# Issuing the half-step products by width: 512-column matmuls first, then 256-column ones

## The chip, the cores and the metric

One Trainium2 chip, one of its cores. The metric is the device time of one execution in microseconds (us). The kernel before took 1057.5 us in the median of three runs (1057.06 to 1058.75).

## What is computed

A decoder trunk of two layers over 256 tokens of width 1024, in float32. Each layer is a half-step SwiGLU, a token mixer (multi-head latent attention in layer 0, forgetting attention in layer 1), a second half-step SwiGLU, and a gated per-layer embedding. The change touches the half-steps alone; there are four of them, and they are most of the arithmetic:

```
D_MODEL = 1024
SEQ = 256
D_FF = 2816

def rms_norm(x, g):
    return (x * lax.rsqrt(jnp.mean(x * x, axis=-1, keepdims=True) + EPS)) * g

def swiglu(x, w_in, w_out):
    gate, up = jnp.split(x @ w_in, 2, axis=-1)
    return (jax.nn.silu(gate) * up) @ w_out

for i in range(DEPTH):
    h = h + FFN_HALF * swiglu(rms_norm(h, g_ffn1[i]), ffn1_w_in[i], ffn1_w_out[i])
    ...                                   # the mixer
    h = h + FFN_HALF * swiglu(rms_norm(h, g_ffn2[i]), ffn2_w_in[i], ffn2_w_out[i])
    gate = jax.nn.sigmoid(rms_norm(h, g_ple[i]) @ ple_w_gate[i])
    h = h + gate * (p[i] @ ple_w_proj[i])
```

## The kernel before

Every operand of a large product is split into two float32r parts, a high one and a low one, and a product is the sum of three: high times high, high weights times low activations, low weights times high activations. An activation tile is laid out as `[128, k, 2, 256]`: for each block `k` of 128 rows the 256 high values and then the 256 low ones. So in a half-step two matmuls do the three products of a block: one streams all 512 columns (high and low) past the high weights (line 241), and one streams the 256 high columns past the low weights (line 242) into the second half of the same 512 columns of PSUM. The trace calls the high weights `whi`, the low ones `wlo`, the activations `xa` (normed input) or `hid` (hidden activations); it names a matmul's moving operand first and its stationary one second.

Weights come in units of 1 MB (eight blocks of 128 rows by 256 columns): SyncE loads a unit into one of three `raw` buffers (line 70); ScalarE copies it into `whi` (line 86) and VectorE subtracts into `wlo` (line 87), in two pieces of four blocks each; `whi` and `wlo` have six buffers each, which are three units. Splitting runs two units ahead of use. A buffer is free again when the last matmul that reads it is done.

A half-step (`ffn`) has two stages. In the first, for each of 11 values of `f`, `part` multiplies `xa` by a unit for the gate (`pg`) and by one for the up path (`pu`): per unit 8 blocks times 2 column groups of 128, so 16 pairs of matmuls, 352 pairs in a half-step. Each accumulates in a PSUM tile of two banks (`pa`, two buffers). ScalarE copies half of the tile out and VectorE adds the other half (`summed`), then come the silu, the product and the split into `hid`. In the second stage, for 4 groups of output columns, `hid` (22 blocks) is multiplied by units of 8, 8 and 6 blocks: 176 pairs in a half-step. The result is added to the residual `h`, and the next norm's `xa` is made of it chunk by chunk (lines 357 and 359); GpSimd sums the squares (lines 367 and 371), and line 377 or 389 spreads their sum with a matmul.

In all half-steps but the first, `f == 0` is issued so that chunks of `xa` may arrive late: blocks 0 to 5 for the gate, blocks 0 to 5 for the up path, then blocks 6 and 7 for the gate, the spreading matmul, blocks 6 and 7 for the up path. In the very first half-step `part` is called with two blocks at a time.

In the half-steps the matmuls stay in the order in which the program issues them (`steady`). VectorE's and ScalarE's instructions are placed by a scheduler, apart from the first few steps of each half-step.

Outside the half-steps, `mm_w` (lines 234 to 236) streams activations of 256 columns past weights, three matmuls to a block, and `mm_x` (lines 247 to 249) streams weights of 256, 384 or 512 columns past activations.

Of the kernel before, what the change touches and what calls it, by code (L numbers as in the profile page):

```python
# [16 lines left out]
P = 128  # L17
S = 256
D = 1024
KD = D // P  # L20
FF = 2816
KF = FF // P
# [129 lines left out]
def trunk(ctx: ExitStack, tc: tile.TileContext, a: dict, out: bass.AP):  # L152
    nc = tc.nc
# [75 lines left out]
    steady = Order(tc)  # L229
# [5 lines left out]
        steady(nc.tensor.matmul(ps, lhsT=hi, rhs=x[:, k, 1, :], start=False, stop=False, skip_group_check=True))  # L235
        return steady(nc.tensor.matmul(ps, lhsT=lo, rhs=x[:, k, 0, :], start=False, stop=stop, skip_group_check=True))  # L236

    def mm_wide(ps, wt, cols, x, k, start, stop):

        hi, lo = wt[0][:, cols], wt[1][:, cols]  # L240
        steady(nc.tensor.matmul(ps, lhsT=hi, rhs=x[:, k], start=start, stop=False, skip_group_check=True))  # L241
        return steady(nc.tensor.matmul(ps[:, 1, :], lhsT=lo, rhs=x[:, k, 0, :], start=False, stop=stop, skip_group_check=True))  # L242

    def mm_x(ps, wt, x, k, tt, start, stop):

# [6 lines left out]
    start = ExitStack()  # L252
# [26 lines left out]
    def small_loads():  # L279
# [22 lines left out]
        out=upper, in_=upper, compare_op=ALU.is_ge, fill=0.0, base=0, pattern=[[1, P]], channel_multiplier=-1  # L302
# [4 lines left out]
        out=mask[:, P:], in_=mask[:, P:], compare_op=ALU.is_ge, fill=NEG, base=0, pattern=[[-1, P]], channel_multiplier=1  # L307
# [23 lines left out]
    def tt_op(o, x, y, op):  # L331
        return nc.vector.tensor_tensor(o, x, y, op=op)  # L332
# [63 lines left out]
    def two(r):  # L396
        return r.unsqueeze(1).broadcast_to([P, 2, S])


    def wide():  # L400
        return pa().rearrange("p (b a t) -> p b a t", b=2, a=2)

    def part(ps, wt, x, ks):
        for k in ks:
            for b in range(2):
                last = mm_wide(ps[:, b], wt(k), slice(b * P, (b + 1) * P), x, k, start=(k == 0), stop=(k == KD - 1))
        return last.ins

    def ffn(norm, after, fpool, beside={}, opened=None):

        steady.on = True
        x = norm.x
        hid = fpool.tile([P, KF, 2, S], F32R, name="hid", tag="hid", bufs=1)
        r = rh = None
        def summed(ps, name):
            o = fpool.tile([P, 2, S], F32, name=name, tag=name)
            nc.scalar.copy(o, ps[:, :, 0, :])
            tt_op(o, ps[:, :, 1, :], o, ALU.add)
            return o
# [5 lines left out]
        def product(f, gt, hf):  # L425
            tt_op(hf, gt, hf, ALU.mult)
            nc.scalar.copy(hid[:, 2 * f : 2 * f + 2, 0, :], hf)
            return tt_op(hid[:, 2 * f : 2 * f + 2, 1, :], hf, hid[:, 2 * f : 2 * f + 2, 0, :].bitcast(F32), ALU.subtract)

        for f in range(KF // 2):  # L430
            if f == 0:
                if opened:
                    pg, pu, pieces, roots, copies = opened
                    gt = summed(pg, "gt")
                    for _ in pieces:
                        pass
                    first = gt, summed(pu, "hf")
                    roots()
                    beside[0](None, None)
                    continue  # L440
                else:
                    pg, wg = wide(), w.get()
                    pu, wu = wide(), w.get()
                    part(pg, wg, x, range(6))
                    part(pu, wu, x, range(6))
                    part(pg, wg, x, range(6, KD))
                    order.on = True
                    r = norm.spread()
                    last = part(pu, wu, x, range(6, KD))
            else:  # L450
                pg = wide()
                if f == 1 and opened:
                    w.get(), w.get()
                part(pg, w.get(), x, range(KD))
                if f == 1 and opened:
                    r = roots()
                    gate(first[0])
                    product(0, *first)
                    copies()
# [5 lines left out]
            if f:  # L465
                pu = wide()
                last = part(pu, w.get(), x, range(KD))
            hf = summed(pu, "hf")
            low = product(f, gt, hf)
# [4 lines left out]
        for dp in range(4):  # L474
            ps = wide()
            for k0 in range(0, KF, 8):
                wt = w.get()
                for k in range(min(8, KF - k0)):
                    for b in range(2):
                        mm_wide(  # L480
                            ps[:, b], wt(k), slice(b * P, (b + 1) * P), hid, k0 + k, start=(k0 + k == 0), stop=(k0 + k == KF - 1)
                        )
            ot = summed(ps, "ot")
            tt_op(ot, ot, two(rh), ALU.mult)
            c = slice(2 * dp, 2 * dp + 2)
            tt_op(h[:, c, :], h[:, c, :], ot, ALU.add)
            after.chunk(dp)
# [785 lines left out]
```

## Time and profile before

| what | value |
|---|---|
| median of three runs | 1057.5 us |
| the profiled execution's own time | 1056.91 us |
| its span, first to last instruction | 1055.2 us |
| TensorE (PE) busy | 1041.4 us, 99% |
| weight loads (PEld) busy | 920.8 us, 87% |
| VectorE (DVE) busy | 783.8 us, 74% |
| ScalarE (ACT) busy | 593.5 us, 56% |
| mean granted TensorE clock | 0.999 |

The profiled execution took 1056.91 us; 1.7 us of it lie around the span. Matmuls are pipelined: the profile draws each longer than the time it holds the array, so their busy times overlap and their sum is more than the span. What one matmul costs is read from start to start of neighbours in the timeline.

### The profile page before, as it was taken

Reading aid. Unit: us, or ns where it says so; the run is one execution under the profiler, and the core shown is the slowest. Engines: PE = TensorE matmul, PEld = TensorE weight load, DVE = VectorE, ACT = ScalarE, POOL = GpSimd, SP = SyncE. Lnnn points to the kernel's source line nnn. Section 1 sums busy time; section 2 is a strip of 40 time slices with the busy share of each in tenths; the row PEclk is TensorE's granted clock in tenths of the full one; section 3 lists DMA queues with packets and bytes.
Section 4 is the critical chain, followed back from the end, with each engine's and each line's share of the span. In section 5 each row is a group of like instructions: output and inputs, shape, how many; then the busy total and the mean of one; then the engine's idle time right before and its main releaser. Section 6 shows DMA issues by size and latency. Waiting matters only on the chain.

```text
span 1055.2 us, 16340 instructions
## 1 busy us (share of the span) xinstructions
PE 1041.4 (99%) x6380; PEld 920.8 (87%) x6380; DVE 783.8 (74%) x1369; ACT 593.5 (56%) x903; POOL 71.7 (7%) x99
## 2 busy tenths in 40 slices
PE   8999999999999999999999999999999999999998
PEld 7888888987898888889988888889998988888886
DVE  5988766679979777666987676658888797766665
ACT  6655554568765555455656555535655665554552
POOL 0000000133110000001110000001000200000010
PEclk9999999999999999999999999999999999999999
DMA  7765555525336665556546554654643356555541
GB/s 241 241 209 190 188 182 170 170 88 183 98 113 198 202 198 189 162 196 211 161 145 218 196 191 154 214 153 140 217 138 115 96 194 215 185 189 182 187 160 40
DMA packets 171105, 182.60 MB, mean 173 GB/s; under 512 B 6094, under 2 KB 164372, under 8 KB 171028
## 3 DMA queue, kind: packets, MB, share of 16 engines
q1 hardware_dynamic: 170452, 181.03, 53.1%
q8 instruction: 50, 0.82, 0.3%
q10 hardware_dynamic: 576, 0.53, 0.2%
q14 instruction: 27, 0.22, 0.1%
HBM read 180.50 MB, written 1.05 MB: 172 GB/s over the span
## 4 chain that ended last, share of the span: by engine, by line
PE 92%; DVE 3%; issue 2%; POOL 1%; ACT 1%; DMA 1%; ACTq 0%; DVEq 0%; POOLq 0%
PE pa L241 45%; PE pa L242 23%; PE pa L247 3%; PE pa L249 3%; PE pa L248 3%; PE pa L234 2%; PE pa L236 2%; PE pa L235 2%; PE pb L601 1%; DVE wlo L87 1%; PE pb L508 1%; PE pb L548 1%; PE pb L536 1%; DMA xn<-in_x_dram 1%; POOL sq L367 1%
## 5 line engine op out<-in xcount | busy, mean ns | idle before, releaser
L87 DVE TENSOR_TENSOR wlo<-raw,whi 128x1024 fp32r<-128x1024 f32 (+2 forms) x351 | 418.2, 1202 | 199.2 <-ACT whi L86 198.6
L86 ACT CAST whi<-raw 128x1024 fp32r<-128x1024 f32 (+2 forms) x351 | 352.6, 1016 | 318.9 <-PE pa L241 195.0
L241 PE MATMUL pa<-xa,whi 128*128 128x512 f32 x1408 | 497.4, 396 | 0.9 <-DVE xa L359 0.9
L242 PE MATMUL pa<-xa,wlo 128*128 128x256 f32 x1408 | 396.2, 281 | 0.0
L241 PEld LDWEIGHTS pa<-xa,whi 128*128 128x128 f32 x1408 | 265.4, 189 | 64.1 <-DVE xa L359 1.2
L242 PEld LDWEIGHTS pa<-xa,wlo 128*128 128x128 f32 x1408 | 264.6, 188 | 0.1
L241 PE MATMUL pa<-hid,whi 128*128 128x512 f32 x704 | 244.2, 393 | 0.0
L242 PE MATMUL pa<-hid,wlo 128*128 128x256 f32 x704 | 195.5, 278 | 0.0
L241 PEld LDWEIGHTS pa<-hid,whi 128*128 128x128 f32 x704 | 131.9, 187 | 30.2
L242 PEld LDWEIGHTS pa<-hid,wlo 128*128 128x128 f32 x704 | 132.3, 188 | 0.0
L367 POOL TENSOR_TENSOR sq<-sq 128x512 f32<-128x512 f32 x21 | 31.6, 1504 | 841.5 <-ACT sq L365 827.7
L247 PE MATMUL pa<-whi,xa 128*128 128x256 f32 (+3 forms) x192 | 58.9, 307 | 0.0
L249 PE MATMUL pa<-whi,xa 128*128 128x256 f32 (+3 forms) x192 | 57.5, 300 | 0.0
L248 PE MATMUL pa<-wlo,xa 128*128 128x256 f32 (+3 forms) x192 | 57.3, 298 | 0.0
L234 PE MATMUL pa<-xa,whi 128*128 128x256 f32 x184 | 54.2, 295 | 0.0
L236 PE MATMUL pa<-xa,wlo 128*128 128x256 f32 x184 | 51.9, 283 | 0.0
L235 PE MATMUL pa<-xa,whi 128*128 128x256 f32 x184 | 51.8, 282 | 0.0
L247 PEld LDWEIGHTS pa<-whi,xa 128*128 128x128 f32 x192 | 36.1, 188 | 1.4 <-issue 0.5
L423 ACT ACTIVATE gt<-gt 128x512 f32<-128x512 f32 x44 | 27.6, 627 | 16.8 <-DVE gt L332 16.8
L248 PEld LDWEIGHTS pa<-wlo,xa 128*128 128x128 f32 x192 | 36.2, 188 | 0.8
L249 PEld LDWEIGHTS pa<-whi,xa 128*128 128x128 f32 x192 | 36.1, 188 | 0.9
L234 PEld LDWEIGHTS pa<-xa,whi 128*128 128x128 f32 x184 | 34.5, 188 | 1.9 <-issue 1.4
(281 smaller groups left out, 1196.9 us busy)
## 6 DMA issues: line engine op xcount, KB each, us to landing
raw<-in_ffn_w_in_dram SPq DMA_DIRECT2D x86, 1024.0 KB, 5.1
raw<-in_ffn_w_out_dram SPq DMA_DIRECT2D x32, 1024.0 KB, 5.1
raw<-in_ffn_w_out_dram SPq DMA_DIRECT2D x16, 768.0 KB, 4.6
raw<-in_ple_w_gate_dram SPq DMA_DIRECT2D x8, 1024.0 KB, 5.2
raw<-in_fox_w_in_dram SPq DMA_DIRECT2D x8, 1024.0 KB, 6.0
raw<-in_mla_w_o_dram SPq DMA_DIRECT2D x4, 1024.0 KB, 5.0
raw<-in_fox_w_o_dram SPq DMA_DIRECT2D x4, 1024.0 KB
raw<-in_mla_w_in_dram SPq DMA_DIRECT2D x3, 1024.0 KB, 6.3
```

The lines of the kernel that those rows point to most:

```text
L86: self.order(self.nc.scalar.copy(h, whole))
L87: self.order(self.nc.vector.tensor_tensor(low, whole, h.bitcast(F32), op=ALU.subtract))
L234: steady(nc.tensor.matmul(ps, lhsT=hi, rhs=x[:, k, 0, :], start=start, stop=False, skip_group_check=True))
L235: steady(nc.tensor.matmul(ps, lhsT=hi, rhs=x[:, k, 1, :], start=False, stop=False, skip_group_check=True))
L236: return steady(nc.tensor.matmul(ps, lhsT=lo, rhs=x[:, k, 0, :], start=False, stop=stop, skip_group_check=True))
L241: steady(nc.tensor.matmul(ps, lhsT=hi, rhs=x[:, k], start=start, stop=False, skip_group_check=True))
L242: return steady(nc.tensor.matmul(ps[:, 1, :], lhsT=lo, rhs=x[:, k, 0, :], start=False, stop=stop, skip_group_check=True))
L247: steady(nc.tensor.matmul(ps, lhsT=x[:, k, 0, t], rhs=wt[0], start=start, stop=False, skip_group_check=True))
L248: steady(nc.tensor.matmul(ps, lhsT=x[:, k, 0, t], rhs=wt[1], start=False, stop=False, skip_group_check=True))
L249: steady(nc.tensor.matmul(ps, lhsT=x[:, k, 1, t], rhs=wt[0], start=False, stop=stop, skip_group_check=True))
L367: nc.gpsimd.tensor_tensor(sq, sq, self.acc, op=ALU.add)
L423: nc.scalar.activation(gt, gt, AF.Silu)
```

## The change

In the half-steps a unit's matmuls are issued in another order. Before, each block and column group had its 512-column matmul and then its 256-column one. After, all 512-column matmuls of the unit (or of the blocks of one call of `part`) come first, and then all 256-column ones. Number, shapes, operands and accumulation are the same. The new line 255 stands for the old 241, and the new 248 for the old 242.

```
-    def mm_wide(ps, wt, cols, x, k, start, stop):
-
-        hi, lo = wt[0][:, cols], wt[1][:, cols]
-        steady(nc.tensor.matmul(ps, lhsT=hi, rhs=x[:, k], start=start, stop=False, skip_group_check=True))
-        return steady(nc.tensor.matmul(ps[:, 1, :], lhsT=lo, rhs=x[:, k, 0, :], start=False, stop=stop, skip_group_check=True))
+    def by_width(pss, wt, x, ks, first, last, at=0):
+        out = None
+        for low in range(2):
+            for k in ks:
+                for b, ps in enumerate(pss):
+                    cols = slice(b * P, (b + 1) * P)
+                    if low:
+                        out = steady(
+                            nc.tensor.matmul(
+                                ps[:, 1, :], lhsT=wt(k)[1][:, cols], rhs=x[:, at + k, 0, :], start=False, stop=(k == last),
+                                skip_group_check=True,
+                            )
+                        )
+                    else:
+                        steady(
+                            nc.tensor.matmul(
+                                ps, lhsT=wt(k)[0][:, cols], rhs=x[:, at + k], start=(k == first), stop=False, skip_group_check=True
+                            )
+                        )
+        return out
...
     def part(ps, wt, x, ks):
-        for k in ks:
-            for b in range(2):
-                last = mm_wide(ps[:, b], wt(k), slice(b * P, (b + 1) * P), x, k, start=(k == 0), stop=(k == KD - 1))
-        return last.ins
+        return by_width([ps[:, b] for b in range(2)], wt, x, ks, 0, KD - 1).ins
...
                 wt = w.get()
-                for k in range(min(8, KF - k0)):
-                    for b in range(2):
-                        mm_wide(
-                            ps[:, b], wt(k), slice(b * P, (b + 1) * P), hid, k0 + k, start=(k0 + k == 0), stop=(k0 + k == KF - 1)
-                        )
+                by_width([ps[:, b] for b in range(2)], wt, hid, range(min(8, KF - k0)), -k0, KF - 1 - k0, k0)
```

TensorE at the start of the third half-step (layer 1, first one), before; `pa_5329` is the gate's PSUM tile, `xa_5101` the activations, `whi_5181` and `wlo_5182` the first piece of the gate's unit:

```order
L236 MATMUL pb_5260<-xa_3346,wlo_5115 128x256
L241 MATMUL pa_5329<-xa_5101,whi_5181 128x512
L242 MATMUL pa_5329<-xa_5101,wlo_5182 128x256
L241 MATMUL pa_5329<-xa_5101,whi_5181 128x512
L242 MATMUL pa_5329<-xa_5101,wlo_5182 128x256
```

The two widths alternate, and go on alternating to the end of the half-step. The same place after the change; `pa_5340` is the up path's tile, `whi_5185` and `wlo_5186` are the gate's second piece, and line 394 is the old 377:

```order
L236 MATMUL pb_5260<-xa_3346,wlo_5115 128x256
L255 MATMUL pa_5329<-xa_5101,whi_5181 128x512 x8
L255 MATMUL pa_5329<-xa_5101,whi_5185 128x512 x4
L248 MATMUL pa_5329<-xa_5101,wlo_5182 128x256 x8
L248 MATMUL pa_5329<-xa_5101,wlo_5186 128x256 x4
L255 MATMUL pa_5340<-xa_5101,whi_5252 128x512 x8
L255 MATMUL pa_5340<-xa_5101,whi_5256 128x512 x4
L248 MATMUL pa_5340<-xa_5101,wlo_5253 128x256 x8
L248 MATMUL pa_5340<-xa_5101,wlo_5257 128x256 x4
L255 MATMUL pa_5329<-xa_5101,whi_5185 128x512 x4
L248 MATMUL pa_5329<-xa_5101,wlo_5186 128x256 x4
L394 MATMUL pb_5407<-ss_5321,mean_d_118 128x256
```

Blocks 4 and 5 (the x4 rows of `whi_5185`, whose activations come from a later chunk) are now reached after eight 512-column matmuls, where eight pairs stood ahead of them. VectorE at the end of the second half-step (layer 0), before; `ot_4947` is the last output tile, `h_158` the residual, `wlo_4964` and `wlo_4968` the two pieces of a unit that is used later:

```order
L87 TENSOR_TENSOR wlo_4964<-raw_4871,whi_4963 128x1024
L87 TENSOR_TENSOR wlo_4968<-raw_4871,whi_4967 128x1024
L332 TENSOR_TENSOR ot_4947<-pa_4828,ot_4947 128x512
L332 TENSOR_TENSOR ot_4947<-ot_4947,rh_3453 128x512
L332 TENSOR_TENSOR h_158<-h_158,ot_4947 128x512
L359 SCALAR_TENSOR_TENSOR xa_3346<-h_158,gvec_147,xa_3346 128x256 x2
```

And after, where line 349 is the old 332 and line 376 the old 359:

```order
L87 TENSOR_TENSOR wlo_4964<-raw_4871,whi_4963 128x1024
L349 TENSOR_TENSOR ot_4947<-pa_4828,ot_4947 128x512
L87 TENSOR_TENSOR wlo_4968<-raw_4871,whi_4967 128x1024
L349 TENSOR_TENSOR ot_4947<-ot_4947,rh_3453 128x512
L349 TENSOR_TENSOR h_158<-h_158,ot_4947 128x512
L376 SCALAR_TENSOR_TENSOR xa_3346<-h_158,gvec_147,xa_3346 128x256 x2
```

One subtraction of a later unit has moved from ahead of the tile's first operation to behind it; the same five operations stand ahead of `xa`.

## Rows read from the trace of the kernel before

**Rows 1.** The page: busy times; granted clock; the chain that ended last.
```profile
PE 1041.4 (99%) x6380; PEld 920.8 (87%) x6380; DVE 783.8 (74%) x1369; ACT 593.5 (56%) x903; POOL 71.7 (7%) x99
...
PEclk9999999999999999999999999999999999999999
...
PE 92%; DVE 3%; issue 2%; POOL 1%; ACT 1%; DMA 1%; ACTq 0%; DVEq 0%; POOLq 0%
```

**Rows 2.** The page's costliest groups: busy and mean ns of one | idle before.
```profile
L241 PE MATMUL pa<-xa,whi 128*128 128x512 f32 x1408 | 497.4, 396 | 0.9 <-DVE xa L359 0.9
...
L241 PE MATMUL pa<-hid,whi 128*128 128x512 f32 x704 | 244.2, 393 | 0.0
```

**Rows 3.** Timeline of TensorE (start us, us), second half-step, first stage.
```profile
349.89 0.39 PE L241 MATMUL pa<-xa,whi 128*128 128x512 f32 x1
...
356.87 0.40 PE L241 MATMUL pa<-xa,whi 128*128 128x512 f32 x1
```

**Rows 4.** The same, third half-step, first stage.
```profile
600.11 0.39 PE L241 MATMUL pa<-xa,whi 128*128 128x512 f32 x1
...
606.47 0.39 PE L241 MATMUL pa<-xa,whi 128*128 128x512 f32 x1
```

**Rows 5.** Busy time by stretch (x: matmuls in it), first stages of all half-steps.
```profile
100.00:135.00 35.00, 35.00 (x199) 30.47 (x198) 25.05 (x30) 19.73 (x26) 0.00 (x0) 1.00 0.54 176
...
335.00:425.00 90.00, 90.00 (x518) 78.83 (x517) 67.29 (x76) 50.70 (x66) 0.00 (x0) 1.00 0.62 203
...
540.00:640.00 100.00, 100.00 (x568) 87.10 (x567) 75.02 (x87) 58.06 (x75) 0.00 (x0) 1.00 0.58 187
...
850.00:940.00 90.00, 90.00 (x518) 78.82 (x517) 69.30 (x81) 52.55 (x68) 0.00 (x0) 1.00 0.58 189
```

**Rows 6.** Timeline of TensorE, first half-step: a transpose between pairs.
```profile
68.40 0.27 PE L317 MATMUL pb<-ident,grow 58*128 58x58 f32 x1
```

**Rows 7.** Timeline of TensorE, first half-step, second stage.
```profile
150.06 0.40 PE L241 MATMUL pa<-hid,whi 128*128 128x512 f32 x1
...
156.65 0.39 PE L241 MATMUL pa<-hid,whi 128*128 128x512 f32 x1
```

**Rows 8.** Timeline of TensorE, a run of 512-column matmuls alone.
```profile
1025.35 0.39 PE L247 MATMUL pa<-whi,xa 128*128 128x512 f32 x1
...
1030.72 0.39 PE L249 MATMUL pa<-whi,xa 128*128 128x512 f32 x1
```

**Rows 9.** The same, 256-column matmuls alone, activations moving.
```profile
200.03 0.28 PE L234 MATMUL pa<-xa,whi 128*128 128x256 f32 x1
...
204.63 0.28 PE L234 MATMUL pa<-xa,whi 128*128 128x256 f32 x1
```

**Rows 10.** The same, 256-column matmuls alone, weights moving.
```profile
722.09 0.28 PE L247 MATMUL pa<-whi,xa 128*128 128x256 f32 x1
...
726.17 0.28 PE L247 MATMUL pa<-whi,xa 128*128 128x256 f32 x1
```

**Rows 11.** Timeline of TensorE, start of the third half-step [idle before <-releaser].
```profile
522.99 0.40 PE L241 MATMUL pa<-xa,whi 128*128 128x512 f32 x1
...
526.83 0.50 PE L241 MATMUL pa<-xa,whi 128*128 128x512 f32 x1 [0.85 <-DVE xa L359]
```

**Rows 12.** The same, at the spreading matmul.
```profile
534.57 0.70 PE L377 MATMUL pb<-ss,mean_d 128*128 128x256 f32 x2 [0.42 <-POOL ss L371]
```

**Rows 13.** Timeline of all engines, end of the second half-step.
```profile
494.69 0.57 ACT L417 COPY ot<-pa 128x512 f32<-128x512 f32 x1
...
494.81 1.23 DVE L87 TENSOR_TENSOR wlo<-raw,whi 128x1024 fp32r<-128x1024 f32 x1 [0.18 <-ACT whi L86]
...
495.96 0.68 DVE L332 TENSOR_TENSOR ot<-pa,ot 128x512 f32<-128x512 f32 x1
```

**Rows 14.** Timeline of all engines, second half-step, first stage.
```profile
349.94 0.58 ACT L417 COPY gt<-pa 128x512 f32<-128x512 f32 x1
...
351.20 0.68 DVE L332 TENSOR_TENSOR gt<-pa,gt 128x512 f32<-128x512 f32 x1
```

## The prediction

> **What bounds the kernel now.** I read the page first. The reader is to see that TensorE is busy 99% of the span, that the chain that ended last is 92% TensorE, and that the granted clock is full throughout, which is the 2.4 GHz level [rows 1]. So an order of matmuls is worth only what it does to the pace of TensorE's own stream, or to the few places where that stream waits. The groups show how much of the stream is changed: 1408 pairs with `xa` moving and 704 with `hid` moving [rows 2].
>
> Durations in those groups (396 and 393 ns) overlap, so I then read starts in the timeline, over long stretches. With `xa` moving, 20 pairs go from 349.89 to 356.87: 349.0 ns a pair [rows 3]. In the third half-step 18 pairs go from 600.11 to 606.47: 353.3 ns [rows 4]. The same instructions thus run at two paces. The busy times by stretch tell where: 518 matmuls in 90 us in the second and in the fourth half-step (two of the 518 began before the stretch, so 258 pairs at 348.8), 568 in 100 us in the third (353.4), 199 in 35 us late in the first (about 355) [rows 5]. In the first half-step the pace changes behind one transpose at 68.4 us, with no change of tiles or shapes [rows 6]. With `hid` moving, 19 pairs go from 150.06 to 156.65: 346.8 ns [rows 7].
>
> At 2.4 GHz the 768 columns of a pair need 320 ns, so every pair has 27 to 33 ns of stall in its stream. What the change can win or lose is a part of these.
>
> **The pace after the change.** It makes runs of one width: 16 matmuls of 512 columns, then 16 of 256 (12 and 12, or 4 and 4, at the edges). The trace of before has runs of one width outside the half-steps. 512 columns with weights moving: 23 matmuls from 1025.35 to 1030.72, 233.5 ns each [rows 8]. 256 columns with activations moving: 39 from 200.03 to 204.63, 117.9 ns [rows 9]. 256 columns with weights moving: 36 from 722.09 to 726.17, 113.3 ns [rows 10].
>
> For `hid` I take 233.5 + 113.3 = 346.8, which is what its pair costs now [rows 7, 8, 10]: 0 us. That `hid` goes with the faster 256-column row is a choice: its pairs alternate at exactly that sum, while `xa`, which is the moving operand of the slower row, alternates above it. Were it 117.9 instead, 704 x 4.6 ns would add 3.2 us.
>
> For `xa` no row shows a run of 512 columns. The 256-column run is the row with the same moving tile: 117.9. For the 512-column run I take the nearest row, 233.5, and so 351.4 a pair. Now: the second and fourth half-step (704 pairs) and the first up to the transpose (five of its 11 steps, 160 pairs) run at 349.0, the other 544 at 353.3; the mean is 350.7. So 1408 x 0.74 ns = **+1.0 us**. The bounds: from below, both widths lose nothing that `xa` adds, 346.8 a pair: 1408 x (346.8 - 350.7) = -5.4 us. From above, the 512-column run loses what the 256-column run loses against weights moving, 4.6 ns a matmul (356.0 a pair, +7.5 us), or twice that as it has twice the columns (360.6, +14.0 us). I keep the middle value because in alternation the 512-column matmul starts its successor after 229 to 236 ns, around 233.5, and the 256-column one carries the rest.
>
> Changes from one width to the other come twice a unit; an alternating order is nothing but such changes, and its pair costs no more than the sum of the two runs [rows 7, 8, 10], so they are put at 0.
>
> **The places where the stream waits.** At the start of the third half-step TensorE begins at 522.99, has eight pairs to do on early chunks, and then waits until 526.83 for block 4 of `xa` from VectorE [rows 11]. After the change it does only eight 512-column matmuls ahead of block 4 and is there at 522.99 + 8 x 0.2335 = 524.86; the eight 256-column ones (0.94 us) move behind the wait. The wait ends with VectorE, so it grows by 0.94 us. At the end of this `f == 0` the spreading matmul now waits 0.42 us for GpSimd's sum [rows 12]; TensorE comes 0.94 us later, so that wait goes. Left over: **+0.5 us**. The second and fourth half-step start the same way, but there no wait stands and blocks 4 and 5 are ready in time: 0, and at most 0.9 us each if they are not.
>
> At the end of a half-step VectorE's chain to the next `xa` gets one subtraction (1.23 us) between its first and second operation. It is not added: now the subtraction stands ahead of the first operation and holds it until 495.96, though ScalarE's copy, which starts at 494.69, is done at 495.26 [rows 13]. Moreover that copy stands behind the `whi` copy of the same piece, whose buffer is now free earlier, as the high weights are read first. I put it at 0, between -0.5 and +0.5 us at each of four ends.
>
> **Buffers.** A unit's `whi` pieces are free after 1.9 and 3.7 us of its 5.6, earlier than now (2.8 and 5.6). The first `wlo` piece is free 1.9 us later (4.7 for 2.8), the second at the end as now; so `raw` buffers and loads, which wait for both pieces, keep their times. Behind a subtraction that waits, VectorE has the PSUM addition that frees a tile. Its cover: the addition of the group that ended just before 349.94 is over at 351.88 [rows 14], and the tile is wanted again one unit later, 16 x 349 ns = 5.6 us after 349.94, at 355.5. The slack of 3.6 us holds two subtractions of 1.2 us. And `wlo` itself is wanted 3.7 us later in its unit than now. So 0; if that cover were gone, each 0.1 us late would cost 8.8 us over the 88 units of the first stages.
>
> **The sum.** 1056.91 (the profiled execution) + 1.0 + 0.5 = 1058.4. That execution lies 0.6 us under the median of the runs shown, so runs should give **1059.0 us**, 0.14% above 1057.5.
>
> **A rule of the skill against the rows.** The 512-column run shows 233.5 ns and the 256-column run 113.3 ns at full clock [rows 8, 10]. The Trainium skill (TensorE: Matmul & The Clock Gate, Back-to-back issue gap) gives the isolated gap as columns over 2.4 GHz plus 2.5 ns: 216 and 109 ns, so long runs of one width would give 325 ns a pair, some 55 us less in all, an estimate by that page. No run of one width in this trace comes near it, and the measurement decides; it stands as the last rival.
>
> **Rivals.**
> - *The long runs pay on `xa` as the short ones do (slower).* Place: the 1408 matmuls of 512 columns with `xa` moving, now in runs of 16, 12 or 4. For it: the only run of one width on `xa` is 4.6 ns a matmul slower than the one on weights [rows 9, 10]. Against it: alternation on `xa` stays at 349.0 in most half-steps, below 351.4. Price 7.5 to 14 us: 1066.5 with 0.5 us from the waits, up to 1073. It decides from 1.5 ns a matmul on. 25%.
> - *Grouping takes the stalls of `xa` away (faster).* For it: the two paces show that the stall depends on how neighbours fall together, not on tiles [rows 3, 4, 6], so a steady run could settle at the pace of `hid`. Against it: the 256-column run on `xa` did not [rows 9]. Price -5.4 + 0.5: 1052.6. A milder form, in which the half-steps that run at 353.3 settle at 351.4 and the others stay at 349.0, gives 544 x -1.9 ns = -1.0 us and counts as no change. 24%.
> - *VectorE's longer wait for the first `wlo` piece reaches TensorE (slower).* Against it stands the slack above; 0.1 us a unit gives 1066.3. 5%.
> - *Stall-free runs.* 320 ns a pair by the clock, 62 us less: 996. Rows 8 to 10 speak against it. 1%.
>
> **Chances and range.** The forecast (1059.0, own range 1057 to 1061) has 45%. No change that this kernel's measurement can tell means within 0.2%, 2.1 us. Of the forecast's 45%, 34 lie within that, 10 above it and 1 below; of the slower two's 30%, 27 lie above and 3 within; of the faster two's 25%, 23 lie below and 2 within. So faster 24%, same 39%, slower 37%. The range reaches to both near rivals: 1052.5 to 1066.5; left out are the upper half of the first rival and the last two.
>
> **What would show it.** The pair as two starts: a 512-column run on `xa` at 233 to 234 ns and a 256-column run at 117 to 118 makes the forecast's step right; 238 or more ns in the long run is the first rival, 113 in the short one the second. `hid` must stay at 347. The first wait of the third half-step should be near 1.8 us and the one at the spreading matmul gone. TensorE waiting on VectorE's `gt` or `hf` additions inside a half-step would make the buffer step wrong, and a granted clock below 2.4 GHz all of it.

## The result and the profile after

The changed kernel took 1049.71 us in the median (1048.28 to 1051.06, five runs), the kernel before 1058.75 beside it (1057.06 to 1059.68, five runs): a ratio of 0.9911, 95% interval 0.9900 to 0.9921. The prediction was 1059.0, with a range down to 1052.5: the change is faster by 9 us and the time lies 2.8 us below the range.

The profiled execution took 1048.94 us with a span of 1047.2. The page of the changed kernel: busy times, the granted clock, and the chain that ended last.

```profile
PE 1033.1 (99%) x6380; PEld 918.7 (88%) x6380; DVE 777.6 (74%) x1369; ACT 599.6 (57%) x903; POOL 77.3 (7%) x99
...
PEclk9999999999999999999999999999999999999999
...
PE 95%; DVE 3%; DMA 1%; issue 0%; ACT 0%; POOL 0%; ACTq 0%; DVEq 0%
```

TensorE is as full as before and its clock is full [rows 1]; the same count of matmuls takes less time, so the pace changed. The pace is read from starts in the timeline of TensorE, second half-step, first stage (start us, us, ..., count of neighbours of one line):

```profile
343.48 1.98 PE L248 MATMUL pa<-xa,wlo 128*128 128x256 f32 x16
345.29 3.82 PE L255 MATMUL pa<-xa,whi 128*128 128x512 f32 x16
348.95 2.05 PE L248 MATMUL pa<-xa,wlo 128*128 128x256 f32 x16
350.84 3.84 PE L255 MATMUL pa<-xa,whi 128*128 128x512 f32 x16
354.51 1.98 PE L248 MATMUL pa<-xa,wlo 128*128 128x256 f32 x16
```

Start to start, the 512-column runs go at 229 ns a matmul (345.29 to 348.95, 350.84 to 354.51), the 256-column runs at 113 (343.48 to 345.29) and 118 (348.95 to 350.84) in turn; the two units together give 344.7 ns a pair where [rows 3] gave 349.0. The second stage of the same half-step:

```profile
443.38 3.82 PE L255 MATMUL pa<-hid,whi 128*128 128x512 f32 x16
447.04 2.08 PE L248 MATMUL pa<-hid,wlo 128*128 128x256 f32 x16
448.95 3.82 PE L255 MATMUL pa<-hid,whi 128*128 128x512 f32 x16
452.60 2.08 PE L248 MATMUL pa<-hid,wlo 128*128 128x256 f32 x16
```

On `hid` it is 228 to 229 (443.38 to 447.04, 448.95 to 452.60) and 119.4 (447.04 to 448.95): 348.0 a pair, where [rows 7] gave 346.8. Over all stages the means (start to start, from the trace, waits and the first microseconds at the lower clock left out) are 229.3 and 115.6 ns on `xa`, 228.5 and 119.5 on `hid`. The start of the third half-step, in the same view:

```profile
517.54 2.00 PE L255 MATMUL pa<-xa,whi 128*128 128x512 f32 x8
521.81 1.19 PE L255 MATMUL pa<-xa,whi 128*128 128x512 f32 x4 [2.27 <-DVE xa L376]
...
529.70 0.59 PE L394 MATMUL pb<-ss,mean_d 128*128 128x256 f32 x2
```

The wait of [rows 11] grew from 0.85 to 2.27 us, and the one at the spreading matmul [rows 12] is gone. The waits of TensorE, all that are over 0.2 us (total, times, longest):

```profile
PE pa L255 <- DVE xa L376: 2.3, 1, 2.3
PE pb L1148 <- DMA xn<-in_x_dram: 2.1, 2, 1.7
PE pb L774 <- POOL zq L827: 1.1, 1, 1.1
PE pb L406 <- POOL ss L388: 1.1, 1, 1.1
PE pb L340 <- DVE idle L273: 1.1, 1, 1.1
PE pb L517 <- ACT qt L615: 0.8, 1, 0.8
```

No wait on `gt` or `hf` is among them. Cut at the first matmul of each stage, the two traces differ so:

| stretch | before us | after us | difference |
|---|---|---|---|
| ahead of the first half-step | 9.90 | 8.41 | -1.49 |
| four first stages (`xa`) | 126.64, 123.83, 126.58, 123.83 | 124.62, 122.49, 124.39, 122.49 | -6.88 |
| four second stages (`hid`) | 60.90, 60.89, 60.90, 60.89 | 61.13 each | +0.94 |
| between the half-steps, and the end | 300.8 | 300.3 | -0.54 |

The first row is the arrival of `x`, which the change doesn't touch; it took 8.5 to 9.2 us in the twelve kernels below that carry no probe, so about one of the 8 us between the two profiles is not the change's. What is: the four `xa` stages. (The medians differ by 9.0 us. The profiled execution of before, 1056.91, lies under all five runs that stand beside the changed kernel.)

### The profile page after: what moved, and what is told of

Same layout as the page of the kernel before. It is cut to its first block, busy times and chain, and to the rows that moved or that the text cites. A ratio compares the mean times of both kernels' runs of the same rounds, so it can differ in the third digit from the quotient of the medians.

```text
span 1047.2 us, 16326 instructions
## 1 busy us (share of the span) xinstructions
PE 1033.1 (99%) x6380; PEld 918.7 (88%) x6380; DVE 777.6 (74%) x1369; ACT 599.6 (57%) x903; POOL 77.3 (7%) x99
## 4 chain that ended last, share of the span: by engine, by line
PE 95%; DVE 3%; DMA 1%; issue 0%; ACT 0%; POOL 0%; ACTq 0%; DVEq 0%
PE pa L255 46%; PE pa L248 24%; PE pa L264 3%; PE pa L266 3%; PE pa L265 3%; PE pa L234 2%; PE pa L236 2%; PE pa L235 2%; DVE wlo L87 1%; PE pb L611 1%; PE pb L518 1%; PE pb L558 1%; PE pb L546 1%; PE pb L517 1%; DMA xn<-in_x_dram 1%; PE pb L266 1%
## 5 line engine op out<-in xcount | busy, mean ns | idle before, releaser
L255 PE MATMUL pa<-xa,whi 128*128 128x512 f32 x1408 | 342.6, 394 | 2.3 <-DVE xa L376 2.3
L255 PEld LDWEIGHTS pa<-xa,whi 128*128 128x128 f32 x1408 | 257.8, 188 | 54.3 <-DVE xa L376 3.5
L248 PEld LDWEIGHTS pa<-xa,wlo 128*128 128x128 f32 x1408 | 177.8, 188 | 8.6
L248 PE MATMUL pa<-xa,wlo 128*128 128x256 f32 x1408 | 179.4, 278 | 0.0
L255 PE MATMUL pa<-hid,whi 128*128 128x512 f32 x704 | 168.7, 391 | 0.0
L248 PEld LDWEIGHTS pa<-hid,wlo 128*128 128x128 f32 x704 | 90.8, 191 | 3.7
L248 PE MATMUL pa<-hid,wlo 128*128 128x256 f32 x704 | 91.9, 283 | 0.0
L349 DVE TENSOR_TENSOR hid<-hf,hid 128x512 fp32r<-128x512 f32 x44 | 30.5, 692 | 29.0 <-ACT hid L441 29.0
L236 PE MATMUL pa<-xa,wlo 128*128 128x256 f32 x184 | 51.9, 283 | 0.0
L431 ACT COPY gt<-pa 128x512 f32<-128x512 f32 x44 | 25.8, 587 | 36.8 <-PE pa L248 36.8
L264 PEld LDWEIGHTS pa<-whi,xa 128*128 128x128 f32 x192 | 36.1, 188 | 1.3 <-issue 0.5
```

Of the source, the lines that this page charges most:

```text
L248: nc.tensor.matmul(ps[:, 1, :], lhsT=wt(k)[1][:, cols], rhs=x[:, at + k, 0, :], start=False, stop=(k == last), skip_group_check=True,)
L255: nc.tensor.matmul(ps, lhsT=wt(k)[0][:, cols], rhs=x[:, at + k], start=(k == first), stop=False, skip_group_check=True)
L264: steady(nc.tensor.matmul(ps, lhsT=x[:, k, 0, t], rhs=wt[0], start=start, stop=False, skip_group_check=True))
```

## The experiments

Every diff is against the changed kernel unless it says otherwise. Paces are start to start, ns a pair of one 512-column and one 256-column matmul. In brackets behind a time stand its ratio to the kernel before, run beside it, and the 95% interval of that ratio. In several of the profiles TensorE's granted clock fell to its lower level for a few microseconds at the start of the third half-step (last section); stage paces are those at the full clock.

**One stage at a time.** `by_width` got an argument for the order; "pair" is the order of before.

```
-   by_width([ps[:, b] ...], wt, hid, ...)                 # e1_first
+   by_width([ps[:, b] ...], wt, hid, ..., order="pair")
-   return by_width([ps[:, b] ...], wt, x, ks, 0, KD - 1)  # e2_second
+   return by_width([ps[:, b] ...], wt, x, ks, 0, KD - 1, order="pair")
```

> Grouping by width in the first stages only (xa moving); the second stages (hid moving) alternate as before. My theory: the gain lies in the 1408 pairs with xa moving, 350.7 to 344.9 ns (1408 x -5.8 = -8.1 us), and the grouped second stage loses, 346.8 to 348.2 ns (704 x 1.4 = 1.0 us). So hid goes back to 346.8 ns a pair, xa stays at 344.9, and the runs come out 1.0 us under the changed kernel's 1049.7: 1048.7. Rival: the pace of hid was moved by what ran ahead of it in the same half-step and not by its own order; then hid stays near 348 and the time at 1049.7.

> Grouping by width in the second stages only; the first stages alternate as before. My theory: xa at 349 to 353 ns a pair as before, hid at 348.2 ns, so 1.0 us over the kernel before: 1059.7. Because xa in alternation has two paces (349.0 and 353.3) and which one a half-step takes may turn out otherwise here, 1055.5 to 1063 is possible without a word on the theory; the hid pace is the test. Rival: hid stays at 346.8 and the time at 1058.7, since its loss came with the grouped first stage.

First stages only: 1053.7 us (before beside it 1058.1; ratio 0.9959, 0.9943 to 0.9975). Second stages only: 1058.5 (1.0007, 0.9997 to 1.0017). `xa` is at 345 to 346 where grouped and `hid` at 348.0 where grouped, as in the changed kernel. But the alternating `hid` did not go back to 346.8. Timeline of TensorE, first stages only grouped, second half-step, second stage (20 pairs between the two rows):

```profile
449.86 0.40 PE L248 MATMUL pa<-hid,whi 128*128 128x512 f32 x1
...
456.93 0.40 PE L248 MATMUL pa<-hid,whi 128*128 128x512 f32 x1
```

That is 353.5 ns, in all four half-steps, with the same instructions at the same SBUF places as before: 704 x 5.3 = 3.7 us over the grouped stage, which accounts for most of the 4 to 5 us by which this run is slower than the changed kernel (by medians and by ratios). So my expectation was wrong, and an alternating stream on `hid` has the same slow rhythm that [rows 4] showed on `xa`. In the second run `xa` alternated at 353 in three half-steps and at 349.5 in one. Grouping `hid` is no loss of 1 us by itself; it is one against a rhythm that happened to be good.

**Neighbours and length of the runs.** The turns of a unit in another order:

```
-   [(low, k, b) for low in range(2) for k in ks for b in bs]
+   [(low, k, b) for k in ks for low in range(2) for b in bs]   # e3_block
+   [(low, k, b) for low in range(2) for b in bs for k in ks]   # e4_column
```

> Order by block: for each block of 128 rows the two 512-column matmuls (both column groups, the same moving operand), then the two 256-column ones; runs of two in place of sixteen, in both stages. Theory A (a matmul is cheaper when its neighbour has just streamed the same moving operand, as both column groups of a block do in the changed kernel): the pace stays, 344.9 ns a pair on xa and 348.2 on hid, and the wait at the start of the third half-step goes back to its old size (-0.9 us): 1048.8. Theory B (the length of a run of one width is what counts, each change of width costs): half of the steps are changes here instead of one in sixteen, so xa comes half way back to its old pace, 347.8 ns: 1053; if only long runs pay, 1057.

> By width as in the changed kernel, but within a width the eight blocks of the first column group and then the eight of the second: no two neighbours share the moving operand, and eight neighbours in a row write the same PSUM bank. Theory A (sharing the moving operand): the 512-column run on xa goes up to 233.5 ns and the 256-column run to 117.9 as in the runs outside the half-steps, which have no sharing: 351.4 ns a pair, 1408 x 6.5 = +9.2 us, 1058.9. Theory B (run length, width): no change on xa, 344.9, 1049.7.

By block: 1050.12 (0.9925, 0.9909 to 0.9940), 345.2 on `xa` and 348.3 on `hid`, as in the changed kernel: runs of two do it. By column: 1052.59 (0.9947, 0.9932 to 0.9961), and the same paces. Its timeline, second half-step:

```profile
346.86 3.82 PE L248 MATMUL pa<-xa,whi 128*128 128x512 f32 x16
350.51 2.05 PE L242 MATMUL pa<-xa,wlo 128*128 128x256 f32 x16
```

228 ns without a shared moving operand, so theory A (sharing) falls; B falls with the run by block. Of the 3 us or so that "by column" lost, 1.8 are waits for late chunks: it reaches block 4 after four 512-column matmuls, and waits 0.9 us more at the third half-step (3.19 for 2.27) and 0.4 at the second and the fourth.

**Entry and start.** Both in `part`'s calls:

```
-   last = part(pu, w.get(), x, range(KD))                       # e6_entry, hid alternating
+   last = part(pu, w.get(), x, range(KD), "pair" if f == KF // 2 - 1 else "width")
-   part(pg, wg, x, range(6))                                    # e7_start, all four calls of f == 0
+   part(pg, wg, x, range(6), "pair")
```

> As the run with only the first stages grouped, but the last unit of each first stage alternates again, so that the alternating hid stage is entered out of an alternating stream as in the kernel before. Theory (an alternating stream falls into one of several rhythms, 346.7, 349 or 353.3 ns a pair, by how it is entered, and keeps it): hid returns to 346.7 and the runs to 1053.7 - 704 x 6.6 ns = 1049.1, and a little more (0.1 to 0.3 us) for the four alternating units on xa. Rival (353.3 came from another cause, such as when the weight pieces of the second stage are split): hid stays at 353.3, 1053.8.

> The changed kernel, but f == 0 of each half-step alternates as before (blocks 4 and 5 are then reached after eight pairs and not after eight 512-column matmuls). Theory: the wait of TensorE at the start of the third half-step falls from 2.4 to 1.0 us and the one at the spreading matmul comes back with 0.4 to 0.5; together 0.9 us won, less 16 to 32 pairs a half-step at 349 to 353 in place of 345 (0.3 to 0.9 us in all): 1049.2 to 1049.7, against 1049.7 of the changed kernel; no difference that can be measured. Rival (the grown wait is worth its whole 1.4 us): 1048.3.

Entry: 1053.73 (0.9942, 0.9929 to 0.9956), as the rival said, but the trace shows both rhythms in one execution, in the first half-step (rows 1 and 2; 20 pairs, 346.5 ns) and in the second (rows 3 and 4; 20 pairs, 353.0):

```profile
149.93 0.39 PE L248 MATMUL pa<-hid,whi 128*128 128x512 f32 x1
...
156.86 0.39 PE L248 MATMUL pa<-hid,whi 128*128 128x512 f32 x1
...
449.72 0.40 PE L248 MATMUL pa<-hid,whi 128*128 128x512 f32 x1
...
456.78 0.40 PE L248 MATMUL pa<-hid,whi 128*128 128x512 f32 x1
```

So the rhythm is not a property of the instructions, and one alternating unit ahead doesn't choose it; what chooses stays open. Start: 1049.79 (0.9901, 0.9886 to 0.9917), no difference from the changed kernel, as expected: the first wait is back at 1.0 us over the pace and the spreading matmul's at 0.6.

**Where the tiles lie.** In the program `xa` starts at a multiple of 256 bytes of SBUF, `hid` and all weights 192 past one. Two runs put this on trial; the tiles are 512 bytes longer and the views start inside them.

```
+   XA_SHIFT = {(0, 0): 32, (2, 0): 48, (0, 1): 64, (2, 1): 16}   # e5_align: elements, by half-step
+   HID_SHIFT = [80, 96, 16, 48]
+   for m in (80, 96, 112, 0, 16, 32, 48, 64):                    # e8_probe, after the last line
+       mms("W", 24, m, 0); mms("n", 24, m, 0)                    # 512 and 256 columns, mov at m, sta at 0
+   ...                                                           # sta moved, narrowed to 64 and 32, one bank
```

> The changed kernel with other places in SBUF for the moving operands: xa starts 128, 192, 256 and 64 bytes past a multiple of 512 in the four half-steps (0 so far), hid 0, 64, 256 and 384 bytes past one (192 so far). Theory (the place of the moving operand sets how often its stream stalls): hid at 0 falls to xa's 344.9 ns a pair, from 348.0, and xa at 192 rises to 348; the other places show which bits count. Rival (the place is irrelevant; hid is dearer because of what is loaded beside it or of its PSUM turn): all four stages of xa stay at 345 and all of hid at 348. Only the pace by stage is read from it; a time of its own is 1047 to 1053.

> The changed kernel, and behind its end runs of 24 matmuls of one width on constant tiles, into a PSUM tile that nobody reads, while the other engines are idle: moving tile at eight places (0 to 448 bytes past a multiple of 512), stationary tile at three, stationary narrowed to 64 and 32 columns, all into one PSUM bank; and two alternating runs. Theory (place of the moving operand): 512 columns settle at 229.3 ns and 256 at 113.3 or 117.8 where it starts at 0, at 226.7 and 119.5 where it starts at 192. Theory (the weight load is what stalls the stream): with 64 or 32 stationary columns the runs fall towards 213 and 107 ns, 512 and 256 columns at 2.4 GHz. Rival (other engines' use of SBUF causes the stalls): with idle engines all runs fall to 213 and 107. The time of its own, some 1155 us, is without meaning.

The probe first. Between its runs nothing else works (busy us and count of PE, PEld, DVE, ACT, POOL; granted clock; DMA):

```profile
1060.00:1180.00 120.00, 120.00 (x692) 102.04 (x692) 0.00 (x0) 0.00 (x0) 0.00 (x0) 1.00 0.00 1
```

Mean ns of one from the ninth matmul of a run on (for the 229, which was still warming up, from the eighteenth), against the distance from the stationary tile to the moving one modulo 256 bytes; pairs of values are runs at two absolute places:

| distance | 512 columns | 256 columns |
|---|---|---|
| 0 | 226.7, 226.6 | 120.0, 120.0 |
| 64 | 229, 233.3 | 117.9, 117.7 |
| 128 | 232.4, 232.4 | 118.7, 118.7 |
| 192 | 233.5, 233.5 | 117.7, 117.9 |
| 0, stationary moved | 226.7 | 119.9 |
| 128, stationary moved | 232.3 | 118.7 |

At 0 and 128, moving the stationary tile by the same amount brings the same value: there it is the distance, not the place of either. At 64 the distance is not all: the second run went at 233 from its first matmul to its last, where the first had settled at 229. With 64 stationary columns (at 64) the runs take 228.5 and 116.7, with 32 they take 231.1 and 116.6, in one PSUM bank 228.9 and 117.7: neither a narrower weight load, nor the banks, nor the idle engines remove the stalls, so both of those rivals fall. In the kernel itself (a single execution, 1054.58 us) a place gave the same pace on either operand: `hid` at distances 64, 128, 64, 192 ran at 345.6, 351.1, 345.6, 346.7 (348.0 at 0 in the changed kernel), and `xa` at 192, 0, 64, 128 at 347.0, 348.0, 345.0, 351.5. The 512-column runs follow the table (229.4 at 64, 232.7 at 128, 233.0 at 192); the 256-column runs at 192 took 114, not the table's 118. Its `hid` at distance 128:

```profile
445.69 3.90 PE L259 MATMUL pa<-hid,whi 128*128 128x512 f32 x16
449.43 2.05 PE L252 MATMUL pa<-hid,wlo 128*128 128x256 f32 x16
451.32 3.89 PE L259 MATMUL pa<-hid,whi 128*128 128x512 f32 x16
```

233.8 and 118 ns, where the changed kernel had 228.5 and 119.4. A finer sweep:

```
+   for d in (0, 1, 2, 4, 8, 12, ..., 60):    # e9_sweep: elements of 4 bytes
+       run(0, 20, 64 + d, 0); run(1, 20, 64 + d, 0)
+   for dh, dl in ((0, 0), (16, 16), (0, 16), (0, 48), (16, 48), (0, 32)):
+       ...                                   # units of 16 and 16, high and low weights at own distances
```

> The changed kernel and, behind its end, runs of 20 matmuls of 512 and then of 256 columns on constant tiles, the moving tile 0, 4, 8, 16, 32, 48 ... 240 bytes past the stationary one modulo 256; then six kinds of unit (16 of 512 columns, 16 of 256, three times) with the 512-column matmuls' weights and the 256-column ones' at different distances. Theory (the distance of moving and stationary tile modulo 256 bytes sets the pace; the first probe gave 226.7 and 120.0 ns at distance 0, 229 or 233.3 and 117.9 at 64, 232.4 and 118.7 at 128, 233.5 and 117.7 at 192): the same four values come again, and distances between them fall between or repeat the nearest of the four in steps of 16 to 64 bytes; a unit with the high weights at 0 and the low ones at 64 comes to 226.7 to 228.6 + 113.3 to 117.8 = 340 to 346 ns a pair. Rival (what counts is the absolute place of each tile): then distances made by moving only the moving tile give other values here than there, as its base has other remainders. Rival (chance: a run's rhythm is set by how it is entered, the place being a stand-in): the same distance gives another value in the sweep than in the first probe. The time of its own is without meaning.

Timeline of TensorE; the 256-column run at distance 0, and the 512- and the 256-column run at 64 and 192:

```profile
1066.69 2.56 PE L1260 MATMUL pa<-mov,sta 128*128 128x256 f32 x20
1069.08 4.89 PE L1262 MATMUL pa<-mov,sta 128*128 128x512 f32 x20
...
1104.31 4.75 PE L1262 MATMUL pa<-mov,sta 128*128 128x512 f32 x20
1108.90 2.52 PE L1260 MATMUL pa<-mov,sta 128*128 128x256 f32 x20
1111.26 4.78 PE L1262 MATMUL pa<-mov,sta 128*128 128x512 f32 x20
...
1160.36 4.83 PE L1262 MATMUL pa<-mov,sta 128*128 128x512 f32 x20
1165.03 2.44 PE L1260 MATMUL pa<-mov,sta 128*128 128x256 f32 x20
1167.31 4.86 PE L1262 MATMUL pa<-mov,sta 128*128 128x512 f32 x20
```

Most values come again: 119.5 at 0, 229.5 and 118.0 at 64, 233.5 at 192. At 192 the 256-column run took 114.0, where the probe had 117.7 and 117.9: two paces at one distance. In between the 512-column runs lie at 231 to 236 and the 256-column ones at 113 to 122.5; the cheapest sum is 344.6 (at 112 bytes), the dearest 358.7 (at 4). No distance is free of stalls. The units at (0, 0) came to 348 to 349 ns a pair and at (64, 64) to 346.5, 343.1, 346.5, which are `hid`'s and `xa`'s paces in the changed kernel, on constant tiles beside idle engines. The unit with high weights at 0 and low ones at 64, of which I had hoped 340 to 346, came to 348.4. The units with high weights at 64 and low ones at 192 show the second pace of the 512-column run at 64:

```profile
1255.09 3.90 PE L1262 MATMUL pa<-mov,sta 128*128 128x512 f32 x16
1258.82 2.04 PE L1260 MATMUL pa<-mov,sta 128*128 128x256 f32 x16
```

That is 233 ns (1255.09 to 1258.82), in all three of them, where the same distance gave 229 in the units at (64, 64). So my theory holds in part and the rival of the entry has its share: the distance does not fix the pace alone. At 192 every 512-column run in any of these traces went at 232 to 234; at 64 it went at 229 in the kernels and in most of the probes' runs, and at 233 in four of them. What chooses there was not tried by itself.

**The place undone and used.** `xa` of the half-steps moved to 192 (in the changed kernel and in the kernel before), and `hid` moved to 64:

```
+   self.x = shifted(32 if which in (0, 2) else 0)   # e11_xa192; e12_before192: the same on before
+   hid = hid[:, 80 : 80 + KF * 2 * S].rearrange(...)  # e10_hid64
```

> The changed kernel with the half-steps' xa moved by 128 bytes, so that it lies 192 bytes past the weights modulo 256: the distance that weights moving past xa have in the 512-column run from which the prediction took 233.5 ns. Theory: 512-column runs on xa go from 229.3 to 233 ns and 256-column runs stay at 113.3 to 117.8, 346.5 to 351 ns a pair, as in the first half-step of the run with other places (349.0): 1408 x 4.1 = +5.8 us, 1055.5, in the range 1052 to 1058; that is, with this place the prediction's step would have held. Rival (the place is not what made the step fail): 1049.7.

> The kernel before (alternating) with xa at the same 192 bytes. Theory: an alternating pair costs the sum of the two runs at its distance or a slower rhythm above it, so here 346.8 to 353 ns; the change would then be worth between +1 and -6 us at this place, and not its 8 to 9 us. Taken in the middle, 350: the kernel before's own time, 1058. Rival (alternating costs 4 to 8 ns a pair more than grouping at any place): 353 to 357, 1061 to 1067.

> The changed kernel with hid moved by 320 bytes, so that it lies 64 bytes past the weights modulo 256, as xa does, and not 0. Theory (distance of moving and stationary tile modulo 256 bytes): the hid stages fall from 348.0 to 345.5 ns a pair, 704 x -2.5 = -1.8 us: 1047.9 against the changed kernel's 1049.7. Rival (places count only in a kernel that is otherwise undisturbed): 1049.7.

`xa` at 192: 1053.2 (0.9939, 0.9925 to 0.9954). Its second half-step:

```profile
346.79 3.89 PE L255 MATMUL pa<-xa,whi 128*128 128x512 f32 x16
350.51 1.98 PE L248 MATMUL pa<-xa,wlo 128*128 128x256 f32 x16
352.33 3.89 PE L255 MATMUL pa<-xa,whi 128*128 128x512 f32 x16
```

The 512-column runs go at 232.5 here and at 233.0 over all, which is the 233.5 of [rows 8] and not 229.3: nothing but the place was changed. It ended below the 1055.5 expected because the 256-column runs go at 114.0 at this distance, in all four half-steps (113.8 in the rows): 347.0 ns a pair and not 351.4. So undoing the place takes back 3 to 3.5 of the 9 us (by the ratios and by the medians); most of the rest of the miss is the 256-column run. The kernel before at 192: 1064.56 (1.0051, 1.0038 to 1.0063); its alternating `xa` ran at 353.2 to 353.3, and its `hid`, untouched, at 353.3 in all four half-steps. Hence at 192 the change would be worth 11 us against this kernel, 3.7 of them (704 x 5.3 ns) in `hid`, and my theory for the alternating order fell: it is not the sum of the two runs. `hid` at 64: 1048.17 (0.9895, 0.9879 to 0.9910), 345.6 in place of 348.0 (344.1 in the first half-step), as expected; against the changed kernel's ratio of 0.9911 the intervals overlap, so that 1.8 us is shown by the stage's pace (60.71 us for 61.13 in three of them) rather than by the time.

**What sets 113 or 118.** At distance 64 the gaps of a 512-column run repeat 226, 229, 232 ns. Counted over all 256-column runs of 8 or more on `xa` in the changed kernel: 43 of 43 whose last gap ahead was 232 go at 113.3, 43 of 43 others at 117.8. To try it, the units were cut, with `hid` at 64:

```
+   part(pg, w.get(), x, range(KD), 16)               # e13_phase: whole, then
+   last = part(pu, w.get(), x, range(KD), 15)        # 15 + 15 and 1 + 1
+   by_width(..., cut=(16, 15, 10)[k0 // 8])
+   ... 15), ... 15), cut=(15, 15, 12)[k0 // 8]       # e14_counter
```

> The run with hid at 64 bytes, and in it every second unit of a first stage is cut into 15 + 15 and 1 + 1 matmuls (512, then 256 columns), units of the second stage into 16, 15 + 1 and 10 + 2. Theory (the 512-column run repeats gaps of 226, 229, 232 ns; behind a 256-column run at 113.3 it starts at 226, behind one at 117.8 with three slower gaps, and a 256-column run goes at 113.3 only where the last gap ahead was 232): 31 of 32 matmuls of the 256-column runs on xa and 41 of 44 on hid go at 113.3, so 1408 x 15/32 x 4.5 = 3.0 us and 704 x 25/44 x 4.5 = 1.8 us are won, 0.5 us is lost in the added changes of width: 1048.2 - 4.3 = 1043.9. Rival (113.3 or 117.8 is chance, or depends on the unit's buffers): the 256-column runs stay mixed, and the added changes cost: 1048 to 1049.

> The same with the cut 15 + 1 in all units of 16 of both stages, and the units of 12 uncut. Theory: a run of 15 behind a 256-column run at 117.8 ends on a gap of 229, so the 256-column runs fall into 117.8 and stay there: 1408 x 16/32 x 4.5 = 3.2 us and 704 x 16/44 x 4.5 = 1.2 us lost against the run with hid at 64 bytes, and 0.5 us in the added changes: 1048.2 + 4.9 = 1053.1. Rival (chance): as the other run, 1048 to 1049.

Timeline of TensorE, second half-step, most runs ending on 232:

```profile
349.60 3.84 PE L248 MATMUL pa<-xa,whi 128*128 128x512 f32 x16
353.28 1.98 PE L242 MATMUL pa<-xa,wlo 128*128 128x256 f32 x16
355.09 3.60 PE L248 MATMUL pa<-xa,whi 128*128 128x512 f32 x15
358.53 1.86 PE L242 MATMUL pa<-xa,wlo 128*128 128x256 f32 x15
360.23 0.39 PE L248 MATMUL pa<-xa,whi 128*128 128x512 f32 x1
```

And in the counter-run:

```profile
347.65 3.61 PE L248 MATMUL pa<-xa,whi 128*128 128x512 f32 x15
351.09 1.93 PE L242 MATMUL pa<-xa,wlo 128*128 128x256 f32 x15
352.86 0.39 PE L248 MATMUL pa<-xa,whi 128*128 128x512 f32 x1
```

113 ns in the first (353.28 to 355.09, 358.53 to 360.23), 118.0 in the second (351.09 to 352.86). The rule held in every such run of both kernels on `xa`: 61 of 61 behind a 232 at 113, 24 of 24 others at 118 in the first; 11 of 11 and 74 of 74 in the counter-run (one run at the lower clock is left out of each). The times: 1047.71 (0.9873, 0.9855 to 0.9892) and 1049.98 (0.9897, 0.9879 to 0.9916). So the cut sets which of the two paces a run takes. The size was over-estimated, 9 us expected between them and 2.3 measured: the fourth half-step of the first kernel never fell into the good phase (118 in both stages), and in three of the four groups of 44 pairs on `hid` the run of 16 stayed outside it. Each of the four runs of the first lies below each of the four of the second, but the intervals of the ratios overlap; it is the paces that show the effect. 1047.71 is the lowest time of all kernels tried, 0.5 us under the run with `hid` at 64, a difference that these runs don't show.

## Why the prediction was wrong

- *What bounds the kernel*: right. Full clock, TensorE full, and only the pace of its stream moved the time.
- *`hid`, 0 us*: measured +0.94 us over the four stages. The sum was nearly right (348.0 for 346.8), its parts not: 228.5 and 119.5 for 233.5 and 113.3. Both rows it was made of had weights moving past `xa`, at distance 192; `hid` lies at 0.
- *`xa`, +1.0 us with bounds from -5.4*: this is the step that failed. Taken out of the stretches, with the waits' +1.0 us removed, the four stages changed by -7.9 us. "For the 512-column run I take the nearest row, 233.5": it measured 229.3, 1408 x -4.2 = -5.9 us. "The 256-column run is the row with the same moving tile: 117.9": it measured 115.6, 1408 x -2.3 = -3.2. With these two the forecast's own sum gives -8.1. The first error is the place: [rows 8] is at distance 192, this run at 64, and the run with `xa` at 192 gave 233.0. The second is that I took one of two paces for a price: at 64 the 256-column run goes at 113.3 or 117.8 by how the run ahead ended. With `xa` at 192 this second error alone remained, 114.0 for 117.9, and the runs took 1053.2 us for the 1059.0 forecast; what chooses between the two paces at 192 was not tried. The lower bound was wrong for the same reason: it assumed that `xa` moving can only add to what weights moving cost.
- *What I had seen and not used*: the two paces of one instruction stream [rows 3, 4] and the flip behind one transpose [rows 6] said that a row's pace is a state. I priced runs by single rows all the same.
- *Alternation*: "its pair costs no more than the sum of the two runs" was read from `hid` alone. On `xa` the profile of before had 353.3 [rows 4], above the 351.4 of the two rows, and the alternating orders tried since ran at 353.3 in most half-steps, on `hid` too.
- *The waits, +0.5*: about +1.0. The spreading matmul's went as forecast. The first grew by 1.42 us for 0.94; the other 0.4 to 0.5 is time that TensorE won ahead of the half-step: the 256-column matmuls there, outside the change, fell from 117.9 into 113.3 ns, and TensorE stood ready at 517.54, 4.27 us ahead of the release for 3.84 before.
- *Ends of half-steps and buffers, 0*: right; no such wait appears.
- *The rivals*: the faster one ("grouping takes the stalls of `xa` away") had the right side and half of the reason: a steady run does settle at another pace, but "not on tiles" fell, since the place of the tiles counts. Its price of -5.4 us on `xa` was too small. The slower ones didn't occur. Two figures were off: the first rival's 7.5 us are counted from the present pace and were added to the forecast, so 1066.5, the top of the range, should have been 1065.5; and 325 ns a pair would be some 51 us less (1408 x 25.7 + 704 x 21.8 ns), not 55. The 216 and 109 ns that the Trainium skill (TensorE: Matmul & The Clock Gate, Back-to-back issue gap) gives for the isolated gap did not appear: the shortest were 226.7 and 113.3.

Open: what chooses between the rhythms of an alternating stream, and between 229 and 233 ns for a 512-column run at distance 64; and why the distance counts.

## What to carry to other kernels

A matmul's pace in a full stream is not a price of its shape: check that the row you borrow has the same distance between moving and stationary tile, and read several runs of it to see whether it has one pace or two. An order of alternating widths can stand in a slow rhythm for a whole stage; here two neighbours of one width were enough to leave it (353.3 to 345 on `xa`), and where the tiles were placed was worth nearly as much (351.5 at 128, 345.0 at 64).

## What the hardware showed that I had not expected

- The distance between the two tiles modulo 256 bytes changes a float32r matmul by up to 10 ns of 230 (226.7 at 0 to 236.5 at 4 bytes for 512 columns), with the other engines idle.
- The stalls were seen at the full clock alone. In the sweep's first matmuls the granted clock is 0.50, the lower level, and 512 columns take 427 ns, which is 512 over 1.2 GHz with nothing added. The Trainium skill (TensorE: Matmul & The Clock Gate, Back-to-back issue gap) gives that quotient for the cold engine, and the trace agrees. The window on them (busy us and count of PE, PEld, DVE, ACT, POOL; granted clock):

```profile
1050.20:1052.20 2.00, 2.00 (x6) 1.59 (x5) 0.00 (x0) 0.03 (x1) 0.00 (x0) 0.50 0.00 0
```

- A wait can cost a second time, by the clock. In the profile of the kernel with `hid` at 64, it fell to 0.50 behind the wait at the start of the third half-step. Its timeline and the window on it:

```profile
521.51 1.60 PE L255 MATMUL pa<-xa,whi 128*128 128x512 f32 x4 [1.83 <-DVE xa L376]
522.91 2.75 PE L248 MATMUL pa<-xa,wlo 128*128 128x256 f32 x12
525.47 2.95 PE L255 MATMUL pa<-xa,whi 128*128 128x512 f32 x12
```

```profile
522.90:525.40 2.50, 2.50 (x13) 2.49 (x12) 1.15 (x2) 1.43 (x3) 0.41 (x2) 0.50 1.05 363
```

The twelve 256-column matmuls took 213 ns each there (522.91 to 525.47), again without a stall, and some 1.2 us more than at the full clock. The clock fell at that place in six more profiles (first stages only, entry, other places, `xa` at 192, and the two with cut units; waits of 1.81 to 2.27 us). It stayed at 1.00 in the changed kernel's own profile (a wait of 2.27 us) and in the run by column (3.19), and in the five with waits of at most 0.91 us. So the longer wait that the change makes there [rows 11] can bring this loss with it, which the changed kernel's own profile does not show; the runs don't show when the clock falls.
